# A trunk kernel with an expert layer: 64 columns of v move from dense products to gathered rows, and the weights are split two blocks at once

## The chip, the cores and the metric

The kernel runs on one core of a Trainium2 chip. The metric is the device time of one execution in microseconds (us), taken as the median of several executions. The profile names the engines PE (matmul; its weight loads are PEld), DVE (vector), ACT (scalar), POOL (GpSimd, which issues the gathers) and SP (which issues the plain loads).

## What is computed

The trunk has a mixing layer (a convolution and a state-space scan), cross attention to 256 memory tokens, an expert layer and a final norm, over 256 tokens of 2048 columns. The change lies in the last part, the expert layer's second half. For every token 8 heads x 16 experts are chosen out of 16384, each with a gate g and an activation act, and their rows of `v_tab` are added up:

```
def block(args):
    xt, it, gt = args
    u = jnp.take(u_tab, it, axis=0)
    act = jax.nn.gelu(jnp.einsum("td,tkd->tk", xt, u))
    v = jnp.take(v_tab, it, axis=0)
    return jnp.einsum("tk,tkd->td", gt * act, v)
...
h = h + peer(hn, peer_w_q[i], peer_keys[i], peer_u[i], peer_v[i])
...
return rms_norm(h, final_norm_g)
```

## The kernel before

The 256 tokens are two tiles of 128 (tt = 0 and 1). The sum over experts is made in two ways at once, split by columns.

**Dense columns.** The first DC = 1472 columns of v are a plain matrix product: W, a 16384 x 256 matrix of weights that is zero except where a token chose an expert, times `peer_v`. W lies ready in SBUF as two tiles, WA for tt = 0 and WB for tt = 1. The loop of lines 1199 to 1220 walks through 128 blocks of 128 experts. For each block ACT rounds 128 columns of WA and WB into `wh` (line 1205), DVE takes the rest into `wl` (line 1206), SP loads 128 rows of v into `vr` (line 1208), ACT rounds them into `vh` and DVE takes the rest into `vl` (`split`, lines 103 and 104). PE then adds three products (wh by vh, wl by vh, wh by vl; lines 1215 to 1217) for each token tile and each of three column pieces of 512, 512 and 448 columns: 18 matmuls a block, added up in PSUM tiles `acc` for the whole loop. `vr` has four buffers, `vh`, `vl`, `wh` and `wl` have two each.

**Gathered columns.** The last GC = 576 columns are gathered: for each of the 128 chosen experts of a token tile POOL issues one indirect DMA of 128 rows into `v` (line 1180, six buffers), and DVE adds them with their coefficients into `accg` (line 1182). That is 256 gathers and 256 additions. The text of the loop asks for them at a rate of (256 + 8) / 128 a block (line 1218).

**The end.** Lines 1222 to 1239 add `acc` to the residual h3 (which lies in used parts of WA and WB), square and sum the rows, take the root (`rstd_of`, line 110), scale and store. Each token tile needs all of its 128 gathers before the root.

**What sets the order.** The text is no order. When the program is built, a scheduler places every instruction on its engine's list by dependences, priorities and a timeline of its own; the chip then runs each engine's list strictly in order. So an instruction that waits holds up all that stands behind it on its engine, and a row that the scheduler placed late is run late, even if its data came long before.

## Time and profile before

| | us |
|---|---|
| median of 3 runs (2063.14 to 2064.17) | 2064.15 |
| the profiled execution, and its span | 2064.74, 2063.0 |
| first and last matmul of the dense products start | 1533.99, 2046.59 |
| busy in the span: PE, DVE, ACT, POOL | 1961.4, 1683.5, 998.2, 777.7 |

The last quarter of the span is the dense and gathered sum with the tail. The chain of work that ended last runs there through PE's `acc` lines, block after block, and behind the last of them mostly through DVE. The span is what lies between the first and the last instruction; the execution's own time is 1.74 us more.

### The profile page before, as it was taken

What the parts mean: (1) busy time and instruction counts of PE and PEld (TensorE: products, weight loads), DVE (VectorE), ACT (ScalarE), POOL (GpSimd) and SP (SyncE); (2) the same over time, 40 slices, a digit from 0 to 9 for tenths busy, and PEclk for the clock granted to TensorE, in tenths of its full rate; (3) what the DMA queues carried; (4) which work ended last, traced back from release to release, by engine and by line L of the source; (5) the groups of instructions that cost most, each with busy time, mean ns of one, the idle gap of its engine ahead of it and who ended that gap; (6) DMA issues with size and microseconds to landing.
All of it is one profiled execution on the core that took longest, in us unless ns stands there. A gap on an engine that the chain in (4) does not pass through costs nothing.

```text
span 2063.0 us, 33320 instructions
## 1 busy us (share of the span) xinstructions
PE 1961.4 (95%) x12361; PEld 1684.1 (82%) x12379; DVE 1683.5 (82%) x2757; ACT 998.2 (48%) x1586; POOL 777.7 (38%) x589
## 2 busy tenths in 40 slices
PE   8899999999999998899999989989999999999996
PEld 7888886786899888788888878867678888888885
DVE  6699999895655557999976666889869899899998
ACT  5775665455544445333333323556564444444444
POOL 1011111000000003444445656453128677677775
PEclk9999999999999999999999999999999999999998
DMA  7888788757855568899999999888539999999996
GB/s 238 204 227 221 202 224 223 226 183 230 276 180 173 168 196 280 273 310 327 318 354 398 406 384 407 282 294 280 172 128 338 364 336 340 343 341 338 337 339 228
DMA packets 203108, 571.78 MB, mean 277 GB/s; under 512 B 31410, under 2 KB 39459, under 8 KB 202818
## 3 DMA queue, kind: packets, MB, share of 16 engines
q1 hardware_dynamic: 135810, 307.48, 44.1%
q0 software_dynamic: 67136, 262.18, 37.8%
q8 instruction: 97, 1.59, 0.3%
q14 instruction: 65, 0.53, 0.1%
HBM read 556.74 MB, written 12.85 MB: 276 GB/s over the span
## 4 chain that ended last, share of the span: by engine, by line
PE 55%; DVE 15%; issue 11%; DMA 9%; POOL 7%; ACT 2%; SPq 0%; POOLq 0%; DVEq 0%; ACTq 0%
PE acc L1216 8%; PE acc L1217 8%; PE acc L1215 8%; POOL u L928 6%; DVE u L930 5%; PE mm L206 4%; PE mm L205 4%; PE mm L207 3%; PE mm L216 3%; PE mm L214 3%; PE mm L215 3%; PE pw L1051 3%; DMA w_lo<-in_w_kv_mem 2%; PE y L1016 1%; DMA xc<-in_mem 1%
## 5 line engine op out<-in xcount | busy, mean ns | idle before, releaser
L1180 POOL DMA_INDIRECT v<-in_peer_v,vidx x256 | 391.2, 1528 | 182.8 <-DVE accg L1182 72.5
L930 DVE SCALAR_TENSOR_TENSOR u<-u,hnF 128x1280 f32<-128x1280 f32 x256 | 387.9, 1518 | 86.2 <-DMA u<-in_peer_u,uidx 85.5
L928 POOL DMA_INDIRECT u<-in_peer_u,uidx x256 | 295.8, 1156 | 330.2 <-DVE u L930 243.3
L975 PE MATMUL sy<-hnT,ut 128*128 128x256 f32 x1536 | 357.6, 385 | 15.4 <-ACT ut L971 15.4
L191 ACT CAST w_hi<-w_raw 128x1024 fp32r<-128x1024 f32 (+2 forms) x228 | 231.3, 1017 | 242.8 <-PE mm L207 118.2
L975 PEld LDWEIGHTS sy<-hnT,ut 128*128 128x128 f32 x1536 | 287.6, 193 | 56.5 <-ACT ut L971 20.7
L196 DVE TENSOR_TENSOR w_lo<-w_raw,w_hi 128x1024 fp32r<-128x1024 f32 (+2 forms) x192 | 226.7, 1183 | 111.4 <-ACT w_hi L191 111.2
L103 ACT CAST vh<-vr 128x1472 fp32r<-128x1472 f32 x128 | 183.3, 1432 | 251.7 <-PE acc L1216 250.2
L1216 PE MATMUL acc<-vh,wl 128*128 128x512 f32 (+1 forms) x768 | 295.4, 385 | 0.3 <-DVE wl L1206 0.3
L1217 PE MATMUL acc<-vl,wh 128*128 128x512 f32 (+1 forms) x768 | 293.7, 385 | 0.1
L216 PE MATMUL mm<-aT_hi,w_lo 128*128 128x256 f32 x960 | 271.9, 290 | 18.8 <-DVE w_lo L196 7.5
L1215 PE MATMUL acc<-vh,wh 128*128 128x512 f32 (+1 forms) x768 | 276.0, 384 | 2.4 <-ACT vh L103 2.4
L214 PE MATMUL mm<-aT_hi,w_hi 128*128 128x256 f32 x960 | 277.1, 291 | 0.8 <-ACT w_hi L191 0.8
L215 PE MATMUL mm<-aT_lo,w_hi 128*128 128x256 f32 x960 | 274.4, 288 | 0.0
L104 DVE TENSOR_TENSOR vl<-vr,vh 128x1472 fp32r<-128x1472 f32 x128 | 216.8, 1694 | 41.9 <-ACT vh L103 41.4
L1182 DVE SCALAR_TENSOR_TENSOR accg<-v,coef,accg 128x576 f32<-128x576 f32 x256 | 208.7, 815 | 6.5 <-DMA v<-in_peer_v,vidx 2.5
L216 PEld LDWEIGHTS mm<-aT_hi,w_lo 128*128 128x128 f32 x960 | 182.8, 193 | 25.2 <-DVE w_lo L196 9.0
L214 PEld LDWEIGHTS mm<-aT_hi,w_hi 128*128 128x128 f32 x960 | 185.7, 194 | 6.6 <-issue 3.7
L215 PEld LDWEIGHTS mm<-aT_lo,w_hi 128*128 128x128 f32 x960 | 186.1, 194 | 3.4 <-issue 2.0
L1216 PEld LDWEIGHTS acc<-vh,wl 128*128 128x128 f32 x768 | 144.6, 188 | 30.9 <-DVE wl L1206 0.7
L1215 PEld LDWEIGHTS acc<-vh,wh 128*128 128x128 f32 x768 | 144.8, 188 | 28.3 <-ACT vh L103 2.6
L1217 PEld LDWEIGHTS acc<-vl,wh 128*128 128x128 f32 x768 | 144.5, 188 | 22.5 <-DVE vl L104 0.9
(383 smaller groups left out, 3187.8 us busy)
## 6 DMA issues: line engine op xcount, KB each, us to landing
vr<-in_peer_v SPq DMA_DIRECT2D x128, 736.0 KB
raw<-in_peer_u SPq DMA_DIRECT2D x128, 384.0 KB
w_raw<-in_w_kv_mem SPq DMA_DIRECT2D x64, 512.0 KB
w_raw<-in_w_in SPq DMA_DIRECT2D x48, 512.0 KB
w_raw<-in_w_out SPq DMA_DIRECT2D x32, 512.0 KB
w_raw<-in_w_q_mem SPq DMA_DIRECT2D x32, 512.0 KB
w_raw<-in_w_o_mem SPq DMA_DIRECT2D x32, 512.0 KB
w_lo<-in_w_kv_mem POOLq DMA_DIRECT2D x24, 512.0 KB, 7.9
```

Source lines behind the costliest of these rows:

```text
L191: S.copy(hi, raw)
L196: V.tensor_sub(lo, raw, hi.bitcast(F32))
L214: PE.matmul(o, wh, ah, start=first and cb % 2 == 0, stop=False, skip_group_check=True)
L215: PE.matmul(o, wh, al, start=False, stop=False, skip_group_check=True)
L216: PE.matmul(o, wl, ah, start=False, stop=last and end, skip_group_check=True)
L928: G.indirect_dma_start(out=u, out_offset=None, in_=a["peer_u"].rearrange("e (q c) -> (e q) c", c=GU), in_offset=bass.IndirectOffsetOnAxis( ...
L930: V.scalar_tensor_tensor(u, u, 1.0, hnF[:, self.tt, :], op0=ALU.mult, op1=ALU.mult, accum_out=self.act[:, j:j + 1])
L975: PE.matmul(ps[:, b % 2, :], ut[:, k, :], hnT[:, k, :], start=k == 0 and b % 2 == 0, stop=k == KD - 1 and b % 2 == 1, skip_group_check=True)
L1180: G.indirect_dma_start(out=v, out_offset=None, in_=table, in_offset=bass.IndirectOffsetOnAxis(ap=vidx[tt][:, j:j + 1], axis=0))
L1215: PE.matmul(o, wh[:, tt, :], vh[:, cs_], start=b == 0, stop=False)
L1216: PE.matmul(o, wl[:, tt, :], vh[:, cs_], start=False, stop=False)
L1217: PE.matmul(o, wh[:, tt, :], vl[:, cs_], start=False, stop=b == NB - 1)
```

## The change

Four things change in the text. GC goes from 576 to 640 and DC from 1472 to 1408, so that the column pieces are 512, 512 and 384, a block of `vr` has 704 KB instead of 736, and a gather 320 KB instead of 288. The weights are rounded and split for two blocks at a time: `wh` and `wl` are tiles of 2 x 128 columns, one for each token tile, in a ring of three buffers each that the two token tiles share. The products of tt = 1 for the last two blocks are written behind the loop. The gathers are asked for at (256 + 16) / 128 a block. Besides, a root of a constant, `eps_j`, is written ahead of the tail, and the option of splitting weights on POOL is gone.

```
--- before.py
+++ after.py
@@ -48,14 +48,14 @@
 DU = KD * P
 DG = D - DU
 GROUPS = ((1, 1, 2, 2, 2), (2, 2, 2, 2))
-GC = 576
+GC = 640
 GU = 64
 DC = D - GC
 COLS = [slice(c, min(c + 512, DC)) for c in range(0, DC, 512)]
 NCH = len(COLS)
 VG_BUFS = 6
 VR_BUFS = 4
-WL_POOL = 0
+WGROUP = 2
 PQ_COLS = (128, 384, 512)
 NWHOLE = 1
 W_IN, W_K, W_V = True, True, True
@@ -105,6 +105,8 @@
 
     def row_bcast(vec):
         return bass.AP(tensor=vec.tensor, offset=vec.offset, ap=[[0, P], [1, D]])
+
+    eps_j = consts.tile([P, 1], F32, name="eps_j")
 
     def rstd_of(dst, ssq, n):
         S.activation(dst, ssq, AF.Sqrt, bias=eps_t[: dst.shape[0]], scale=1.0 / n)
@@ -1196,28 +1198,41 @@
 
     gathering = gathered()
     done = 0
+
+    def products(b, tt, wh, wl, vh, vl):
+        for c, cs_ in enumerate(COLS):
+            o = acc[tt][:, c, :cs_.stop - cs_.start]
+            PE.matmul(o, wh, vh[:, cs_], start=b == 0, stop=False)
+            PE.matmul(o, wl, vh[:, cs_], start=False, stop=False)
+            PE.matmul(o, wh, vl[:, cs_], start=False, stop=b == NB - 1)
+
+    late = []
     for b in range(NB):
         if b == TAIL_AT:
             load_tail()
-        wh = vs.tile([P, NTT, P], F32R, name="wh")
-        wl = vs.tile([P, NTT, P], F32R, name="wl")
-        for tt in range(NTT):
-            S.copy(wh[:, tt, :], W[tt][:, b, :])
-            (G if tt < WL_POOL else V).tensor_sub(wl[:, tt, :], W[tt][:, b, :], wh[:, tt, :].bitcast(F32))
+            S.activation(eps_j, eps_t, AF.Sqrt)
+        i = b % WGROUP
+        if i == 0:
+            wh, wl = ([vs.tile([P, WGROUP, P], F32R, name=nm, bufs=3) for _ in range(NTT)] for nm in ("wh", "wl"))
+            for tt in range(NTT):
+                w = W[tt][:, b:b + WGROUP, :]
+                S.copy(wh[tt], w)
+                V.tensor_sub(wl[tt], w, wh[tt].bitcast(F32))
         vr = vraw_p.tile([P, DC], F32, name="vr")
         SY.dma_start(vr, a["peer_v"][b * P:(b + 1) * P, :DC])
         vh = vs.tile([P, DC], F32R, name="vh")
         vl = vs.tile([P, DC], F32R, name="vl")
         split(vh, vl, vr)
-        for tt in range(NTT):
-            for c, cs_ in enumerate(COLS):
-                o = acc[tt][:, c, :cs_.stop - cs_.start]
-                PE.matmul(o, wh[:, tt, :], vh[:, cs_], start=b == 0, stop=False)
-                PE.matmul(o, wl[:, tt, :], vh[:, cs_], start=False, stop=False)
-                PE.matmul(o, wh[:, tt, :], vl[:, cs_], start=False, stop=b == NB - 1)
-        while done * NB < (b + 1) * (NTT * NSLOT + 8) and done < NTT * NSLOT:
+        products(b, 0, wh[0][:, i, :], wl[0][:, i, :], vh, vl)
+        if b < NB - 2:
+            products(b, 1, wh[1][:, i, :], wl[1][:, i, :], vh, vl)
+        else:
+            late.append((b, 1, wh[1][:, i, :], wl[1][:, i, :], vh, vl))
+        while done * NB < (b + 1) * (NTT * NSLOT + 16) and done < NTT * NSLOT:
             next(gathering)
             done += 1
+    for x in late:
+        products(*x)
 
     sts = [small.tile([P, NCH + 3], F32, name="rms_st") for _ in range(NTT)]
     for tt, st in enumerate(sts):
```

What the build makes of it is seen in the engines' lists. Up to the first split of the weights they are the same but for one place: on ACT the root into `eps_j` and a table load for it stand at the very start of the kernel, the later table load for Exp (line 314 after) is new, and the table load of the tail is still there.

DVE, a steady block before (names with their numbers: `vl` is the split of a block, `accg1` the sum of the second token tile, `v` a gathered buffer):

```order
L104 TENSOR_TENSOR vl_18857<-vr_18854,vh_18856 128x1472
L1206 TENSOR_TENSOR wl_18849<-WA_8439,wh_18848 128x128
L1206 TENSOR_TENSOR wl_18849<-WB_7774,wh_18848 128x128
L1182 SCALAR_TENSOR_TENSOR accg1_14570<-v_18626,coef1_8417,accg1_14570 128x576
L1182 SCALAR_TENSOR_TENSOR accg1_14570<-v_18659,coef1_8417,accg1_14570 128x576
L104 TENSOR_TENSOR vl_18893<-vr_18890,vh_18892 128x1472
```

The same place after, somewhat more than two blocks:

```order
L104 TENSOR_TENSOR vl_18676<-vr_18673,vh_18675 128x1408
L1184 SCALAR_TENSOR_TENSOR accg1_14571<-v_17939,coef1_8418,accg1_14571 128x640
L104 TENSOR_TENSOR vl_18714<-vr_18711,vh_18713 128x1408
L1184 SCALAR_TENSOR_TENSOR accg1_14571<-v_17942,coef1_8418,accg1_14571 128x640
L1220 TENSOR_TENSOR wl_18706<-WB_7775,wh_18704 128x256
L1220 TENSOR_TENSOR wl_18764<-WA_8440,wh_18762 128x256
L1184 SCALAR_TENSOR_TENSOR accg1_14571<-v_17977,coef1_8418,accg1_14571 128x640
L104 TENSOR_TENSOR vl_18741<-vr_18738,vh_18740 128x1408
L1184 SCALAR_TENSOR_TENSOR accg1_14571<-v_17980,coef1_8418,accg1_14571 128x640
L1184 SCALAR_TENSOR_TENSOR accg1_14571<-v_18007,coef1_8418,accg1_14571 128x640
L104 TENSOR_TENSOR vl_18773<-vr_18770,vh_18772 128x1408
L1184 SCALAR_TENSOR_TENSOR accg1_14571<-v_18010,coef1_8418,accg1_14571 128x640
```

Before, each block has two additions of gathered rows and two splits of weights. After, the splits come once in two blocks, and in every four blocks there are seven additions, six of them seen here.

DVE, the end of the list before, around the root of the first token tile (`accg_14569` is that tile's sum, `accg_14570` the second's):

```order
L1182 SCALAR_TENSOR_TENSOR accg_14570<-v,coef_8417,accg_14570 128x576
L111 RECIPROCAL rms_st<-rms_st 128x1
L1182 SCALAR_TENSOR_TENSOR accg_14570<-v,coef_8417,accg_14570 128x576
L1237 SCALAR_TENSOR_TENSOR WA<-accg_14569,rms_st,WA 128x576
L1237 SCALAR_TENSOR_TENSOR WA<-WA,rms_st 128x512 x2
L1182 SCALAR_TENSOR_TENSOR accg_14570<-v,coef_8417,accg_14570 128x576
L1228 TENSOR_REDUCE rms_st<-rms_st 128x1
L111 RECIPROCAL rms_st<-rms_st 128x1
L1237 SCALAR_TENSOR_TENSOR WB<-accg_14570,rms_st,WA 128x576
L1237 SCALAR_TENSOR_TENSOR WB<-WB,rms_st,WA 128x512 x2
```

And after (`accg_14570` is the first tile's sum, `accg_14571` the second's):

```order
L113 RECIPROCAL rms_st<-rms_st 128x1
L1184 SCALAR_TENSOR_TENSOR accg_14571<-v,coef_8418,accg_14571 128x640
L1252 SCALAR_TENSOR_TENSOR WA<-accg_14570,rms_st,WA 128x640
L1252 SCALAR_TENSOR_TENSOR WA<-WA,rms_st 128x512 x2
L1184 SCALAR_TENSOR_TENSOR accg_14571<-v,coef_8418,accg_14571 128x640 x29
L1243 TENSOR_REDUCE rms_st<-rms_st 128x1
L113 RECIPROCAL rms_st<-rms_st 128x1
L1252 SCALAR_TENSOR_TENSOR WB<-accg_14571,rms_st,WA 128x640
L1252 SCALAR_TENSOR_TENSOR WB<-WB,rms_st,WA 128x512 x2
```

Behind the last `vl`, before has eight additions (three at once, then five singly among the rows of the tail), after has 35 (two, then four singly, then the 29 in one row here, all of the second token tile, whose root stands behind them). Up to the last `vl` it is 248 before and 221 after.

PE, where block 127 follows block 126, before (`acc_14567` is the first token tile's sum, `acc_14568` the second's), from the last row of block 126 on:

```order
L1217 MATMUL acc_14568<-vl_19133,wh_19124 128x448
L1215 MATMUL acc_14567<-vh_19162,wh_19154 128x512
L1215 MATMUL acc_14568<-vh_19162,wh_19154 128x512
L1216 MATMUL acc_14567<-vh_19162,wl_19155 128x512
L1217 MATMUL acc_14567<-vl_19163,wh_19154 128x512
L1215 MATMUL acc_14567<-vh_19162,wh_19154 128x512
L1216 MATMUL acc_14567<-vh_19162,wl_19155 128x512
L1217 MATMUL acc_14567<-vl_19163,wh_19154 128x512
L1215 MATMUL acc_14567<-vh_19162,wh_19154 128x448
L1216 MATMUL acc_14567<-vh_19162,wl_19155 128x448
L1217 MATMUL acc_14567<-vl_19163,wh_19154 128x448
L1216 MATMUL acc_14568<-vh_19162,wl_19155 128x512
```

And after, with `acc_14568` the first token tile's sum and `acc_14569` the second's, from the last rows of block 126 on the first tile to the second row of block 127:

```order
L1206 MATMUL acc_14568<-vh_18884,wl_18876 128x384
L1207 MATMUL acc_14568<-vl_18885,wh_18874 128x384
L1206 MATMUL acc_14569<-vh_18884,wl_18877 128x512
L1207 MATMUL acc_14569<-vl_18885,wh_18875 128x512
L1205 MATMUL acc_14569<-vh_18884,wh_18875 128x512
L1206 MATMUL acc_14569<-vh_18884,wl_18877 128x512
L1207 MATMUL acc_14569<-vl_18885,wh_18875 128x512
L1205 MATMUL acc_14569<-vh_18884,wh_18875 128x384
L1206 MATMUL acc_14569<-vh_18884,wl_18877 128x384
L1207 MATMUL acc_14569<-vl_18885,wh_18875 128x384
L1205 MATMUL acc_14568<-vh_18899,wh_18874 128x512
L1206 MATMUL acc_14568<-vh_18899,wl_18876 128x512
```

In both the second token tile's products of a block follow at once on the first tile's: block 126's second tile stands ahead of block 127, though the text puts it behind.

## Rows read from the trace of the kernel before

**Rows 1.** Stretch of the stage: its length, busy PE, PEld, DVE, ACT, POOL; clock, DMA
```profile
1900.00:1960.00 60.00, 60.00 (x272) 50.88 (x271) 54.90 (x76) 27.60 (x46) 46.63 (x31) 1.00 0.94 334
```

**Rows 2.** Chain of waits near the end: start, us, what
```profile
2031.01 0.47 PE acc L1215 x2
...
2032.62 0.20 PE acc L1215
...
2033.23 0.23 PE acc L1216
...
2042.97 0.47 PE acc L1215 x2
```

**Rows 3.** Timeline of DVE, one block: start, us, what, idle time before it
```profile
1801.08 1.69 DVE L104 TENSOR_TENSOR vl<-vr,vh 128x1472 fp32r<-128x1472 f32 x1 [0.30 <-ACT vh L103]
1802.69 0.28 DVE L1206 TENSOR_TENSOR wl<-WA,wh 128x128 fp32r<-128x128 f32 x1
...
1803.10 1.67 DVE L1182 SCALAR_TENSOR_TENSOR accg<-v,coef,accg 128x576 f32<-128x576 f32 x2
1805.11 1.69 DVE L104 TENSOR_TENSOR vl<-vr,vh 128x1472 fp32r<-128x1472 f32 x1 [0.34 <-ACT vh L103]
```

**Rows 4.** Timeline of all engines at the end
```profile
2042.30 2.52 DVE L1182 SCALAR_TENSOR_TENSOR accg<-v,coef,accg 128x576 f32<-128x576 f32 x3
2045.22 1.82 DVE L1225 TENSOR_TENSOR WA<-WA,acc 128x512 f32<-128x512 f32 x3 [0.41 <-PE acc L1217]
2046.59 0.36 PE L1217 MATMUL acc<-vl,wh 128*128 128x448 f32 x1
2052.86 0.81 DVE L1237 SCALAR_TENSOR_TENSOR WA<-accg,rms_st,WA 128x576 f32<-128x576 f32 x1
2054.91 0.81 DVE L1182 SCALAR_TENSOR_TENSOR accg<-v,coef,accg 128x576 f32<-128x576 f32 x1
```

**Rows 5.** Timeline of PE in an earlier stage, matmuls of 256 columns
```profile
641.03 0.28 PE L216 MATMUL mm<-aT_hi,w_lo 128*128 128x256 f32 x1
...
642.95 0.28 PE L214 MATMUL mm<-aT_hi,w_hi 128*128 128x256 f32 x1
```

**Rows 6.** Groups by line and shape from 1440 us on: busy, mean ns | idle
```profile
L1237 DVE SCALAR_TENSOR_TENSOR WA<-WA,rms_st 128x512 f32<-128x512 f32 x2 | 1.4, 746 | 0.0
L1237 DVE SCALAR_TENSOR_TENSOR WA<-accg,rms_st,WA 128x576 f32<-128x576 f32 x1 | 0.8, 812 | 0.0
L1225 DVE TENSOR_TENSOR WA<-WA,acc 128x512 f32<-128x512 f32 x2 | 1.3, 684 | 0.4 <-PE acc L1217 0.4
L1225 DVE TENSOR_TENSOR WA<-WA,acc 128x448 f32<-128x448 f32 x1 | 0.6, 614 | 0.0
```

**Rows 7.** The page's costliest groups, gathers and the rounding of v
```profile
L1180 POOL DMA_INDIRECT v<-in_peer_v,vidx x256 | 391.2, 1528 | 182.8 <-DVE accg L1182 72.5
L103 ACT CAST vh<-vr 128x1472 fp32r<-128x1472 f32 x128 | 183.3, 1432 | 251.7 <-PE acc L1216 250.2
```

**Rows 8.** Timeline of POOL at the start of the stage
```profile
1538.79 0.95 POOL L1180 DMA_INDIRECT v<-in_peer_v,vidx  x1 [0.31 <-issue]
1540.05 0.95 POOL L1180 DMA_INDIRECT v<-in_peer_v,vidx  x1 [0.30 <-DVE accg L1182]
1541.30 0.95 POOL L1180 DMA_INDIRECT v<-in_peer_v,vidx  x1 [0.30 <-issue]
```

**Rows 9.** DMA issues from 2038 us on: KB each, median us to landing
```profile
v<-in_peer_v,vidx POOLq DMA_INDIRECT x5, 4.0
```

**Rows 10.** Timeline of ACT at the kernel's start
```profile
14.93 0.20 ACT L312 ACTIVATE dtt<-ldt 32x2 f32<-32x2 f32 x1
19.46 0.64 ACT L253 ACTIVATE sqj<-xc 128x512 f32<-128x512 f32 x1 [4.33 <-DMA xc<-in_x]
```

**Rows 11.** Busy time of each engine while u's rows are gathered
```profile
1340.00:1360.00 20.00, 19.94 (x252) 16.68 (x251) 20.00 (x32) 12.05 (x22) 9.29 (x10) 1.00 0.94 320
```

**Rows 12.** Timeline of POOL in that stretch
```profile
1346.48 0.94 POOL L928 DMA_INDIRECT u<-in_peer_u,uidx  x1 [1.07 <-DVE u L930]
```

## The prediction

> **What bounds the kernel now.** I read the stretches of the last stage first. In 60 us of it PE is busy for all 60, at full clock, DVE for 54.9, and the DMA engines move 334 GB/s [rows 1]. So PE sets the pace there, with DVE close behind it. The chain of waits gives the pace: three blocks of v take 2042.97 - 2031.01 = 11.96 us, 3.987 us a block [rows 2]. In it seven matmuls of 512 columns take 1.61 us (0.230 each) and the next three, of 448, take 0.61 us (0.203 each). DVE's row of one block is a split of v that holds it for 1.61 us (1801.08 to 1802.69), two splits of weights for 0.41, two additions of gathered rows for 1.67, then a wait of 0.34 for the next `vh` [rows 3]. That is 3.69 of 3.99 us. Last I read the tail. The last product starts at 2046.59 and ends about 2046.8; call that E. DVE adds up the first token tile from 2045.22 on, scales it from 2052.86 on, adds its last gathered row at 2054.91 = E + 8.1, and the span ends 8.1 us behind that [rows 4]. Before E only PE counts; behind it only DVE's list, and what that waits for.
>
> **The narrower dense products.** Six of a block's 18 matmuls go from 448 to 384 columns. Their price lies between two rows: 16 matmuls of 256 columns follow one another in 1.92 us, 0.120 each [rows 5], those of 448 take 0.203, so a column costs 0.083 / 192 = 0.434 ns, and 384 columns take 0.1755. That also shows that the weight load in between is no floor at 384, since it is none at 256. By the step from 448 to 512 a column costs 0.42 ns, which gives 20.5 us in all; I take the rows around 384: 6 x 0.0278 = 0.167 us a block, 3.82 instead of 3.987, and 128 x 0.167 = **21.3 us** off PE. All of it lies on the path as long as nothing else in the block needs 3.82 us.
>
> **Does DVE keep up?** 64 columns cost DVE 66 to 70 ns [rows 6]. So the split of v falls to 1.54 us, an addition rises to 0.90, and one split of 256 weight columns in place of two of 128 takes 0.205 + 0.14 = 0.345, twice in two blocks, so 0.345 a block instead of 0.41. The list after has 7 additions in 4 blocks, not 8: 1.54 + 0.345 + 1.75 x 0.90 = 3.46 us. DVE keeps up with 0.36 us to spare. What makes that room is that the list puts 27 additions fewer ahead of the last split of v (221 for 248), and those come back below. Bytes change little: 721 KB of `vr` and 1.75 x 328 KB gathered are 1.294 MB in 3.82 us, 339 GB/s, for 334 measured now [rows 1].
>
> **A new wait on ACT.** The two token tiles' `wh` share a ring of three buffers. The WA tile of the next pair therefore waits for the end of the odd block, where PE last reads the WB tile three places before it. Behind it on ACT stands the `vh` of the pair's second block, behind that DVE's `vl`, behind that PE. From the end of the odd block on: about 0.1 us to wake, at most 0.4 for the rounding of 256 columns, 1.4 for `vh` [rows 7], 0.3 to DVE's start [rows 3], 1.54 for `vl`, 3.7 us in all. PE wants that `vl` at the fifth matmul of the next block, 3.82 + 4 x 0.23 = 4.74 us later. The wait is covered by a block of PE's work, with 1 us left, and I set it at nothing. If that cover were gone, a pair would lose up to the rounding, 0.35 us, 64 times: 22 us.
>
> **The last two blocks by token tile** change nothing: PE's list still has the second tile of block 126 ahead of block 127, so the first tile's sum ends about 1.6 us ahead of E, as now (2045.22 is 1.6 us before 2046.8). Cost 0.
>
> **The early root** stands at the kernel's start and spares no table load in the tail. It adds a load there, ahead of Exp at 14.93, where ACT then idles 4.33 us for a DMA [rows 10]. It would have to be longer than that to be seen; without the idle time it would cost its whole length. Cost 0.
>
> **The gathered rows end later, not sooner.** Between E and the end of the first tile's scaling both lists have four single additions, so DVE is through with it at E + 8.1 to E + 8.2 in either. Before, one addition is left then. After, 29 are, with the second tile's root behind them. The six `v` buffers hold landed rows by then, so six additions run at 0.90 us. The seventh needs a gather that can start only when the first frees its buffer, at E + 9.1. POOL issues a gather every 1.25 us when nothing holds it (1538.79, 1540.05, 1541.30: 0.95 of work and 0.30 between) [rows 8], and DVE frees buffers faster than that. So the 23rd gather starts at E + 9.1 + 22 x 1.25 = E + 36.6. In the tail a gather lands 4.0 us from its issue [rows 9], 4.1 with 320 KB; the ring of six stands 6 x 1.25 - 0.9 = 6.6 us of that, so landing does not set the pace. The last addition starts at E + 40.7 instead of E + 8.1: 32.6 us later, and 0.2 more for its width and those of the square and scaling behind it: **32.8 us** on the path.
>
> Bounds of this term. Below: DVE alone, 28 x 0.90 behind E + 8.2, last start E + 33.4, 25.5 us. Above: the mean gather of the loaded stage, 1.53 + 0.30 = 1.83 us [rows 7], 22 of them: 45.5 us. I take 1.25: nothing but gathers is loaded by then, and 328 KB in 1.25 us are 262 GB/s, well under the 334 of the stage [rows 1], so nothing should hold POOL back.
>
> **The sum:** -21.3 + 32.8 = +11.5 us on the profiled execution, 2064.74 to 2076.2. The median of the runs is 0.6 us lower, so I forecast 2075.7, rounded to **2076 us**, 0.6% slower.
>
> **Rivals.**
> 1. *The gathers in the tail keep their loaded pace* of 1.83 us. For it: it is the mean of 256. Against it: those stood behind loads of `vr`. It gives 2064.15 - 21.3 + 45.5 = 2088.
> 2. *DVE sets the tail's pace.* For it: DVE has the work in a row. Against it: no two gathers in the trace start closer than 1.25 us. 2064.15 - 21.3 + 25.5 = 2068.4, at the edge of what can be told from no change.
> 3. *ACT's wait reaches PE* (above). For it: three buffers for two tiles. Against it: 1 us of cover. 2076 + 22 = 2098.
> 4. *DVE's additions hold up POOL.* If an addition, which reads two tiles in SBUF, kept POOL from starting, a gather would take up to 0.9 us more: 22 x 0.9 = 20 us, 2096. Against it: while u's rows are gathered DVE is busy for 20.00 of 20 us with an operation of that form, two inputs in SBUF [rows 11], and a gather takes 0.94 us [rows 12], as it does beside a mostly idle DVE [rows 8]. The Trainium skill ("SBUF — State Buffer", section "Who interferes with whom") has a rule that a vector instruction with two SBUF inputs contends with a GpSimd instruction that reads SBUF, the later of the two blocking fully; rows 11 and 12 do not show it for gathers.
> 5. *The other side: the gathers keep the text's rate*, 2.125 a block, and end at block 121. DVE would need 1.54 + 0.345 + 2.125 x 0.90 = 3.80 us, just under 3.82, and the tail would lose its five additions and the wait for the last, some 5 us: 2064.15 - 21.3 - 5 = 2038. The sign turns where DVE's list has some 26 additions or fewer behind the last split, since 11.5 us are 9 gathers of 1.25 us less than the 35. Against it: the list has 35, and the list of before agrees with its trace (three additions from 2042.30 on, then singly).
>
> **How the numbers follow.** Forecast 0.75; rival 1 0.10; 2 0.04; 3 0.03; 4 0.03; 5 0.05. About 0.2% (4 us) is what a measurement of this kernel can tell from no change. Rival 5 is faster, 0.05; half of rival 2 is the same and the rest, 0.93, slower; I put 0.03 on the same for small errors of both large terms that add up, and leave 0.92. The forecast's own range is 2072 to 2081 (1.25 to 1.45 us a gather, 1 us of PE's term either way). To hold 8 in 10 it reaches to rival 2 below and rival 1 above: 2068 to 2088.
>
> **What would show it.** PE's blocks 3.82 us apart with `acc` never waiting for `vl` or `wl`; the last product 21 us earlier, about 2025.5; then some 29 additions in a row on DVE, the first six back to back, the rest 1.25 us apart and waiting for the DMA of `v`; POOL's gathers 0.95 us long there; the span's end 49 us behind the last product, where it is 16 now. Wrong would be: gathers over 1.4 us long in the tail, blocks longer than 3.9 us, or a list on the chip without the long run of additions.

## The result

Over four runs each the changed kernel takes 2082.7 us (2081.4 to 2084.9) and the kernel before 2063.6 (2062.5 to 2064.2): 1.0089 times as long, 95% interval 1.0073 to 1.0105. It is slower by 19 us, where 12 were forecast. The forecast's sign and place hold: PE needs less time and the tail grows by more than that. But each of the two terms was off, and one reason given for the tail was wrong.

The profiled run of after took 2084.86 us with a span of 2083.1. Its first product of `acc` and its last ones, in PE's row of operations (start, duration, engine, line, operation, idle time ahead of it and what ended it):

```profile
1536.65 0.50 PE L1205 MATMUL acc<-vh,wh 128*128 128x512 f32 x1 [2.24 <-ACT vh L103]
...
2031.67 0.33 PE L1205 MATMUL acc<-vh,wh 128*128 128x384 f32 x1
2031.84 0.34 PE L1206 MATMUL acc<-vh,wl 128*128 128x384 f32 x1
2032.02 0.34 PE L1207 MATMUL acc<-vl,wh 128*128 128x384 f32 x1
```

Matmuls of 384 columns start 0.17 to 0.18 apart, so E, the end of the products, is 2032.2 here (2046.8 before, by [rows 4]). DVE's row behind it is what the prediction described, a run of additions that wait for `v`:

```profile
2039.37 1.41 DVE L1252 SCALAR_TENSOR_TENSOR WA<-WA,rms_st 128x512 f32<-128x512 f32 x2
2040.69 4.56 DVE L1184 SCALAR_TENSOR_TENSOR accg<-v,coef,accg 128x640 f32<-128x640 f32 x5
2046.28 0.89 DVE L1184 SCALAR_TENSOR_TENSOR accg<-v,coef,accg 128x640 f32<-128x640 f32 x1 [1.03 <-DMA v<-in_peer_v,vidx]
...
2074.96 0.88 DVE L1184 SCALAR_TENSOR_TENSOR accg<-v,coef,accg 128x640 f32<-128x640 f32 x1 [0.26 <-issue]
2076.74 0.16 DVE L1243 TENSOR_REDUCE rms_st<-rms_st 128x1 f32<-128x4 f32 x1 [0.90 <-ACT WB L1242]
```

The stretches of the stage answer [rows 1]. Columns are the stretch, the busy time of PE, its weight loads, DVE, ACT and POOL, then granted clock, DMA share and GB/s. The last row is the tail, where PE does nothing for 35 us:

```profile
1800.00:1900.00 100.00, 100.00 (x471) 86.23 (x470) 89.66 (x99) 45.81 (x54) 64.55 (x45) 1.00 0.93 339
2040.00:2075.00 35.00, 0.00 (x0) 0.00 (x0) 25.49 (x31) 0.00 (x0) 24.36 (x24) 0.50 0.82 259
```

So a profiled run falls into three parts: up to the stage's first product, from there to E, and from E to the end of the span. The table has them for all profiles, in us; "behind" is how many additions stand behind the last split of `v` in DVE's order. The first three columns are of the one profiled run of a kernel, the last is the median of its runs. For x4 the two differ most: its profiled run took 2090.6 us, 8 more than the median.

| kernel | first product | to E | tail | behind | median of runs |
|---|---|---|---|---|---|
| before | 1534.0 | 512.8 | 16.2 | 8 | 2063.6 |
| after | 1536.7 | 495.5 | 50.9 | 35 | 2082.7 |
| x1 width alone | 1532.3 | 496.2 | 54.9 | 33 | 2084.4 |
| x2 pairs alone | 1535.3 | 513.7 | 17.2 | 10 | 2067.4 |
| x3 two a block | 1532.1 | 521.7 | 13.9 | 2 | 2069.3 |
| x4 three loads | 1536.3 | 538.6 | 14.0 | 0 | 2082.8 |
| x5 second tile later | 1534.6 | 498.6 | 14.0 | 2 | 2046.0 |
| x6 x1, sum in PSUM | 1532.8 | 496.5 | 46.9 | 32 | 2078.9 |
| x7 x5, sum in PSUM | 1533.0 | 498.5 | 14.0 | 2 | 2047.6 |
| x8 x5 with 576 | 1534.4 | 515.3 | 14.0 | 2 | 2065.2 |
| x9 x5, late blocks | 1530.8 | 499.5 | 10.7 | 2 | 2044.0 |
| x10 x5 with 704 | 1531.7 | 476.9 | 14.0 | 2 | 2027.2 |
| x11 x9 with 704 | 1534.9 | 478.6 | 12.6 | 2 | 2027.3 |

The runs of the kernel before that stand beside the experiments have medians of 2063.2 to 2064.5 and spread from 2059 to 2071, so each experiment's ratio to them is given below, with its 95% interval. How far apart blocks are is taken from the starts of successive roundings of `v` into `vh`. In the code cuts `...` marks lines left out.

### The profile page after: what moved, and what is told of

Its sections match the earlier page's. It is cut to its first block, busy times and chain, and to the rows that moved or that the text cites. A ratio compares the mean times of both kernels' runs of the same rounds, so it can differ in the third digit from the quotient of the medians.

```text
span 2083.1 us, 32994 instructions
## 1 busy us (share of the span) xinstructions
PE 1942.8 (93%) x12361; PEld 1673.4 (80%) x12379; DVE 1682.0 (81%) x2629; ACT 987.5 (47%) x1460; POOL 739.0 (35%) x589
## 3 DMA queue, kind: packets, MB, share of 16 engines
q1 hardware_dynamic: 135810, 303.29, 42.8%
## 4 chain that ended last, share of the span: by engine, by line
PE 53%; DVE 15%; issue 12%; DMA 10%; POOL 7%; ACT 2%; SPq 0%; POOLq 0%; DVEq 0%; ACTq 0%
PE acc L1207 8%; PE acc L1206 8%; PE acc L1205 8%; POOL u L930 7%; DVE u L932 5%; PE mm L218 4%; PE mm L217 3%; PE mm L216 3%; PE mm L208 3%; PE mm L207 3%; PE mm L209 3%; PE pw L1053 3%; DMA w_lo<-in_w_kv_mem 2%; DMA xc<-in_mem 1%; PE y L1018 1%
## 5 line engine op out<-in xcount | busy, mean ns | idle before, releaser
L1182 POOL DMA_INDIRECT v<-in_peer_v,vidx x256 | 359.2, 1403 | 238.0 <-DVE accg L1184 138.3
L930 POOL DMA_INDIRECT u<-in_peer_u,uidx x256 | 289.0, 1129 | 337.4 <-DVE u L932 252.3
L1205 PE MATMUL acc<-vh,wh 128*128 128x512 f32 (+1 forms) x768 | 288.5, 376 | 2.9 <-ACT vh L103 2.9
L1206 PE MATMUL acc<-vh,wl 128*128 128x512 f32 (+1 forms) x768 | 287.6, 375 | 0.0
L1207 PE MATMUL acc<-vl,wh 128*128 128x512 f32 (+1 forms) x768 | 277.7, 375 | 2.1 <-DVE vl L104 2.1
L103 ACT CAST vh<-vr 128x1408 fp32r<-128x1408 f32 x128 | 175.9, 1374 | 145.0 <-PE acc L1206 137.9
L104 DVE TENSOR_TENSOR vl<-vr,vh 128x1408 fp32r<-128x1408 f32 x128 | 208.0, 1625 | 37.0 <-ACT vh L103 33.9
L1184 DVE SCALAR_TENSOR_TENSOR accg<-v,coef,accg 128x640 f32<-128x640 f32 x256 | 225.5, 881 | 14.9 <-DMA v<-in_peer_v,vidx 9.4
```

The lines of the kernel that those rows point to most:

```text
L930: G.indirect_dma_start(out=u, out_offset=None, in_=a["peer_u"].rearrange("e (q c) -> (e q) c", c=GU), in_offset=bass.IndirectOffsetOnAxis( ...
L1182: G.indirect_dma_start(out=v, out_offset=None, in_=table, in_offset=bass.IndirectOffsetOnAxis(ap=vidx[tt][:, j:j + 1], axis=0))
L1184: V.scalar_tensor_tensor(accg[tt], v, coef[tt][:, j:j + 1], accg[tt], op0=ALU.mult, op1=ALU.add)
L1205: PE.matmul(o, wh, vh[:, cs_], start=b == 0, stop=False)
L1206: PE.matmul(o, wl, vh[:, cs_], start=False, stop=False)
L1207: PE.matmul(o, wh, vl[:, cs_], start=False, stop=b == NB - 1)
```

## The experiments

**x1: the width alone.**

```diff
-GC = 576
+GC = 640
```

> The kernel before with 640 gathered columns for 576 and nothing else of the change. Its order has 33 additions behind the last split of v (8 before the change, 35 after it). My theory: each addition behind the end of PE's products costs one issue of a gather, 1.25 us (1.33 as the tail of the changed kernel measured), and the width gives PE's gain. So blocks 3.82 to 3.84 us apart, the last product some 15 us earlier than before, and the time 2.5 us under the changed kernel's 2082.7, since two additions are fewer: 2080. Rival (the weights split two blocks at once cost PE something through their shared ring of three): then PE's blocks are shorter here than the changed kernel's 3.836, and the time is 2076 or less. Rival (the long run of additions comes of the paired splits): then the time is near 2050, which the order speaks against.

Measured: 2084.4 us, 1.0082 (1.0053 to 1.0112), where 2080 were forecast. To E it needs 496.2 us, as the changed kernel does (495.5). So the paired splits give PE nothing and take nothing, and the 64 columns alone bring both the gain and the run of additions. But the tail is 4 us longer than after's, with two additions fewer. Its gathers start 1.65 us apart (20 intervals from 2037.99 to 2070.89), against 1.33 in after (22 intervals from 2041.84 to 2071.03). POOL's row of that tail, then DVE's of the same time:

```profile
2051.30 1.41 POOL L1180 DMA_INDIRECT v<-in_peer_v,vidx  x1 [0.30 <-issue]
2053.01 1.57 POOL L1180 DMA_INDIRECT v<-in_peer_v,vidx  x1 [0.30 <-DMA v<-in_peer_v,vidx]
2054.89 0.95 POOL L1180 DMA_INDIRECT v<-in_peer_v,vidx  x1 [0.30 <-issue]
2056.14 1.37 POOL L1180 DMA_INDIRECT v<-in_peer_v,vidx  x1 [0.30 <-issue]
...
2051.01 0.88 DVE L1182 SCALAR_TENSOR_TENSOR accg<-v,coef,accg 128x640 f32<-128x640 f32 x1 [0.83 <-DMA v<-in_peer_v,vidx]
2052.86 0.88 DVE L1182 SCALAR_TENSOR_TENSOR accg<-v,coef,accg 128x640 f32<-128x640 f32 x1 [0.97 <-DMA v<-in_peer_v,vidx]
2054.07 0.89 DVE L1182 SCALAR_TENSOR_TENSOR accg<-v,coef,accg 128x640 f32<-128x640 f32 x1 [0.33 <-DMA v<-in_peer_v,vidx]
2055.80 0.88 DVE L1182 SCALAR_TENSOR_TENSOR accg<-v,coef,accg 128x640 f32<-128x640 f32 x1 [0.85 <-DMA v<-in_peer_v,vidx]
```

Read them in pairs. The gather of 2053.01 starts while the addition of 2052.86 has 0.73 us to go, and takes 1.57. That of 2056.14 finds 0.54 us left and takes 1.37. That of 2054.89 finds 0.07 left and takes 0.95. All 18 gathers from 2043 on fit 0.95 us plus what is left of the running addition, less about 0.1. This is rival 4, which the prediction had all but thrown out (0.03).

**x2: the paired splits alone.**

```diff
+WGROUP = 2
...
-        wh = vs.tile([P, NTT, P], F32R, name="wh")
...
+        if i == 0:
+            wh, wl = ([vs.tile([P, WGROUP, P], F32R, name=nm, bufs=3) for _ in range(NTT)] for nm in ("wh", "wl"))
...
```

> The kernel before with the weights split two blocks at once and nothing else of the change. Its order has 10 additions behind the last split of v, 8 before. My theory: the shared ring of three weight tiles costs PE nothing, blocks stay 3.987 us apart, and two more additions in the tail cost 2 x 1.3 us: 2063.6 + 2.6 = 2066. Rival (ACT's wait for the ring reaches PE): up to 0.35 us in each of 64 pairs, 2066 + 22 = 2088, with PE waiting at the first matmul of every second block. On the 2.7 us by which the changed kernel was late already ahead of the stage: this kernel has no early square root, so if that caused them, the stage's first product starts at 1534.0 as before; if they are spread between executions, it may start anywhere from 1533 to 1537.

Measured: 2067.4 us, 1.0000 (0.9984 to 1.0017), so no difference that can be told. PE waits for nothing from 1540 on, and blocks are 3.987 us apart but for the first ten (4.07). The tail is 1.0 us longer for two more additions. The stage starts at 1535.3 without an early root. Over all 13 profiles the start lies between 1530.8 and 1536.7; nine with the root average 1533.8, four without it 1533.6. So the 2.7 us by which the profiled run of after was late ahead of the stage are spread between executions.

**x3: two additions behind every split.** DVE's order is fixed as the loop is written, and the loop hands out two gathers a block.

```diff
+    in_order.enter_context(tc.manual_schedule(engines={mybir.EngineType.DVE}))
     for b in range(NB):
...
-        while done * NB < (b + 1) * (NTT * NSLOT + 16) and done < NTT * NSLOT:
+        while done * NB < (b + 1) * (NTT * NSLOT) and done < NTT * NSLOT:
```

> The changed kernel with DVE's order in the last stage written out: behind every split of v two additions of gathered rows, so that 2 stand behind the last split instead of 35. Nothing else differs. My theory: DVE needs 1.625 + 0.345 + 2 x 0.881 = 3.73 us a block, by the means of the changed kernel, PE 3.836, so the blocks stay as they are, the last product starts near 2032, and the tail falls from 50.7 us behind it to about 9 (no gather left to wait for): 2082.7 - 41 = 2042, faster than both. Rival (DVE or the gathers can't hold two a block beside everything else): the blocks lengthen to the 3.99 of before or more, the last product ends near 2052 and the time is 2062 or later. Rival (the loss sits in wider gathers and additions as such, not in their place): 2070 or later.

Measured: 2069.3 us, 1.0019 (1.0005 to 1.0033); the forecast of 2042 failed. The tail shrank as expected, from 50.9 to 13.9 us. But blocks are 4.04 us apart, and DVE's row of two blocks says why:

```profile
1801.03 0.42 DVE L1222 TENSOR_TENSOR wl<-WA,wh 128x256 fp32r<-128x256 f32 x1
1802.25 0.45 DVE L1222 TENSOR_TENSOR wl<-WB,wh 128x256 fp32r<-128x256 f32 x1 [0.80 <-ACT wh L1221]
1802.62 1.61 DVE L104 TENSOR_TENSOR vl<-vr,vh 128x1408 fp32r<-128x1408 f32 x1
1804.16 1.79 DVE L1184 SCALAR_TENSOR_TENSOR accg<-v,coef,accg 128x640 f32<-128x640 f32 x2
1805.87 1.62 DVE L104 TENSOR_TENSOR vl<-vr,vh 128x1408 fp32r<-128x1408 f32 x1
1807.40 1.80 DVE L1184 SCALAR_TENSOR_TENSOR accg<-v,coef,accg 128x640 f32<-128x640 f32 x2
1809.12 0.42 DVE L1222 TENSOR_TENSOR wl<-WA,wh 128x256 fp32r<-128x256 f32 x1
...
1809.90 0.41 ACT L1221 CAST wh<-WB 128x256 fp32r<-128x256 f32 x1 [1.13 <-PE acc L1207]
```

From 1801.03 to 1809.12 there is no idle time but 0.80 us: 7.29 us of work and a wait for the second tile's `wh`, which ACT rounds only when PE has released a buffer of the ring of three. That is the wait of rival 3, reaching PE by another engine: with DVE's order fixed, the next split of `v` queues behind it.

**x4: three buffers for the loads of v.** By the order this makes the additions run ahead, 2.3 a block, and end at block 112.

```diff
-VR_BUFS = 4
+VR_BUFS = 3
```

> The changed kernel with three buffers for the loads of v instead of four. By the order this makes additions run ahead: 2.3 a block up to block 112 and none behind that, so none stands behind the last split. My theory: up to block 112 DVE needs 1.625 + 0.345 + 2.29 x 0.881 = 3.99 us and sets the pace, then PE with 3.83: 112 x 3.99 + 16 x 3.83 = 508 us for the stage instead of 495.5, last product near 2044.5, tail 9 us: 2055. So slower than the order with two a block by some 12 us and faster than both kernels. Rival (four buffers are needed to hide the loads of v): PE waits for vh on a DMA, blocks above 4.1 us, 2070 or later. Rival (only PE's pace and the number behind the end count, DVE's load doesn't): 2042, as the order with two a block.

Measured: 2082.8 us, 1.0084 (1.0060 to 1.0107); the forecast of 2055 failed by 28. No addition is left in the tail, and the stage takes 43 us longer than after's in the profiled run (the slowest of four; by the medians some 8 us less). POOL's gathers and DVE's work of one stretch:

```profile
1803.46 1.23 POOL L1182 DMA_INDIRECT v<-in_peer_v,vidx  x1 [0.30 <-issue]
1805.61 2.09 POOL L1182 DMA_INDIRECT v<-in_peer_v,vidx  x1 [0.92 <-DVE accg L1184]
1808.00 1.41 POOL L1182 DMA_INDIRECT v<-in_peer_v,vidx  x1 [0.31 <-DVE accg L1184]
...
1805.25 1.62 DVE L104 TENSOR_TENSOR vl<-vr,vh 128x1408 fp32r<-128x1408 f32 x1
1806.79 2.72 DVE L1184 SCALAR_TENSOR_TENSOR accg<-v,coef,accg 128x640 f32<-128x640 f32 x3
...
1813.79 0.89 DVE L1184 SCALAR_TENSOR_TENSOR accg<-v,coef,accg 128x640 f32<-128x640 f32 x1 [0.48 <-DMA v<-in_peer_v,vidx]
```

Ten gathers start in 18.46 us (1798.87 to 1817.33), 1.85 us each; 2.29 of them a block make 4.23 us, about what the blocks take (3.9 to 4.7 in stretches of ten up to block 110). The gathers are late because DVE holds them up (that of 1805.61 starts 0.36 us into a split of 1.62), and the additions, which stand ahead of the next split, wait for them, 27 us in all between 1540 and 2010 where after has 2.4. Loads of `v` are waited for once, 2.3 us; whether three buffers cost something besides was not separated.

**x5: the second tile's split behind the next split of v.** In x3's order one step moves.

```diff
...
-                V.tensor_sub(wl[tt], w, wh[tt].bitcast(F32))
+                if tt == 0:
+                    V.tensor_sub(wl[tt], w, wh[tt].bitcast(F32))
...
         split(vh, vl, vr)
+        if i == 0:
+            V.tensor_sub(wl[1], w, wh[1].bitcast(F32))
...
```

> As x3 (two additions behind every split of v, 2 behind the last), with one step of DVE moved: the weight split of the second token tile stands behind the next split of v, no longer ahead of it. In x3 DVE's list is 7.28 us of work for two blocks and a wait of 0.80 for the second tile's rounded weights, which ACT can round only when PE is through with the first tile's old ones (three buffers for both): 8.08 us, PE's 7.67 is no longer the bound. My theory: that wait is what made x3 slow. Behind the next split the weights are there, DVE needs 7.28 for two blocks, PE sets the pace again with 3.836 a block, 495.5 us from the first to the last product, and x3's tail of 13.9 us: 2045, faster than both kernels. Rival (the bytes are the bound: 721 + 656 = 1377 KB a block): at the 355 GB/s that x3 reached in its fastest 100 us a block takes 3.88 us, 2051; at the 343 GB/s of the changed kernel 4.01 us, 2068, and the split of v waits for a DMA. Rival (gathers held up by DVE come too late for two a block): DVE waits for v at its additions.

Measured: 2046.0 us, 0.9912 (0.9890 to 0.9933), faster than both kernels, and 2045 were forecast. Blocks are 3.836 us apart from the eleventh on. DVE's row again:

```profile
1807.68 0.42 DVE L1223 TENSOR_TENSOR wl<-WA,wh 128x256 fp32r<-128x256 f32 x1
1808.25 1.62 DVE L104 TENSOR_TENSOR vl<-vr,vh 128x1408 fp32r<-128x1408 f32 x1 [0.15 <-ACT vh L103]
1809.84 0.42 DVE L1230 TENSOR_TENSOR wl<-WB,wh 128x256 fp32r<-128x256 f32 x1
1810.19 1.80 DVE L1184 SCALAR_TENSOR_TENSOR accg<-v,coef,accg 128x640 f32<-128x640 f32 x2
```

The stretches, with the columns as above:

```profile
1600.00:1700.00 100.00, 100.00 (x471) 86.19 (x470) 95.46 (x105) 45.26 (x53) 79.89 (x53) 1.00 0.98 375
1800.00:1900.00 100.00, 100.00 (x471) 86.19 (x470) 95.66 (x106) 45.24 (x53) 79.83 (x53) 1.00 0.97 361
```

The wait of 0.80 is gone, PE is busy throughout with DVE at 95.5%, and the DMA engines move 361 to 375 GB/s. So neither the bytes nor the gathers bind here. Only the first ten blocks are slow (4.34 each, 5 us in all): the first addition waits 3.10 us for its start value from memory and the second 2.18 us for its gather, and in a fixed order the splits wait behind them.

**x6 and x7: the running sum in PSUM**, in x1 and in x5.

```diff
+    accp = psg.tile([P, 1024], F32, name="accp")[:, :GC]
...
+            V.tensor_copy(accp, accg[tt])
...
-                V.scalar_tensor_tensor(accg[tt], v, coef[tt][:, j:j + 1], accg[tt], op0=ALU.mult, op1=ALU.add)
+                V.scalar_tensor_tensor(accp, v, coef[tt][:, j:j + 1], accp, op0=ALU.mult, op1=ALU.add)
+                if j == NSLOT - 1:
+                    V.tensor_copy(accg[tt], accp)
```

> x1 (the kernel before with 640 gathered columns), with the running sum of the gathered rows held in PSUM instead of SBUF: an addition then reads one tile in SBUF and one in PSUM, and 32 stand behind the last split. In x1's tail a gather takes 0.95 us plus what is left of the addition that DVE is in the middle of when it starts (1.47 with 0.66 us left, 0.95 with 0.07), 1.73 us from start to start. Theory (an addition that reads two tiles in SBUF holds up a gather that starts behind it; the rule of the Trainium skill, SBUF - State Buffer, Who interferes with whom): here no gather of the tail is longer than about 0.96 us, they start 1.25 apart, and 19 x 0.48 = 9 us and one addition go: 2074. Rival (the tail's gathers are slowed by memory or by their queue): they keep 1.1 to 1.57 us and the time is 2082 or more. The predicted text had thrown this cause out.

> x5 with the running sum in PSUM as in x6. If PE sets x5's pace: 2045 as x5, within 2 us, with gathers of 0.95 us wherever no split of v runs at their start. If x5 waits for gathers that DVE holds up: faster than x5 by that wait. If an addition that reads PSUM is slower than 0.88 us by more than 0.1, DVE passes PE's pace and it is slower than x5.

Measured for x6: 2078.9 us, 1.0075 (1.0053 to 1.0097), 5.5 us under x1 and 5 over the forecast of 2074; in the profiles the tail is 8.0 us shorter. The forecast's 9 us for the gathers took 19 steps of 1.73 us; by x1's 20 steps of 1.65 it is 20 x 0.40 = 8, and the one addition less is nearly made up for by a copy of 0.82. POOL's and DVE's rows of its tail:

```profile
2054.44 0.95 POOL L1184 DMA_INDIRECT v<-in_peer_v,vidx  x1 [0.30 <-issue]
2055.69 0.95 POOL L1184 DMA_INDIRECT v<-in_peer_v,vidx  x1 [0.30 <-issue]
...
2060.69 0.94 POOL L1184 DMA_INDIRECT v<-in_peer_v,vidx  x1 [0.30 <-issue]
...
2060.15 1.81 DVE L1186 SCALAR_TENSOR_TENSOR accp<-v,coef,accp 128x640 f32<-128x640 f32 x2 [0.69 <-DMA v<-in_peer_v,vidx]
```

The last 20 gathers all take 0.94 to 0.96 us, and from 2040.66 on they start 1.25 apart, whatever DVE is doing. One that starts 0.54 us into an addition (2060.69, the first of the two additions from 2060.15 on) takes 0.94 too. In x6's stage the splits of `v`, whose two inputs are still in SBUF, go on holding gathers up (2.13 us at 1900.51, 1.30 us ahead of a split's end). The same engine, the same instruction and the same bytes: what decides is whether DVE's running instruction reads two tiles in SBUF. (x6 moves what the addition writes out of SBUF as well. That this is not it is seen in the kernel before, at `H<-H,y`, further down: it reads one tile in SBUF and writes one, and holds no gather up.) That is the rule of the Trainium skill ("SBUF — State Buffer", section "Who interferes with whom"): a vector instruction with two SBUF inputs and a GpSimd instruction that reads SBUF contend, and the later one blocks. The traces agree where the gather is the later one, 0.95 us without and up to 1.57 with it in the tail. They do not show it the other way round: an addition that starts while a gather runs keeps its 0.88 to 0.89 us.

x7 takes 2047.6 us, 0.9915 (0.9889 to 0.9942), as x5: there PE sets the pace, and gathers held up a little cost nothing. An addition takes 0.886 us with its sum in PSUM and 0.882 without.

**x8: x5's order with the 576 columns of before.**

```diff
-GC = 640
+GC = 576
```

> x5 with the 576 gathered columns of before: pairs of blocks and DVE's order as there, no column moved. PE needs 3.987 us a block, 512.8 us in all; 754 + 590 = 1344 KB a block are 337 GB/s. Theory (PE sets the pace in both): last product where before has it, tail 13.9 instead of 16.3 us, 2062; and the distance to x5 is what the 64 columns are worth when the additions keep up, 17 us (128 x 0.15 less what the tail's width costs). Rival (the bytes are the bound): x5 and this come within 8 us of each other.

Measured: 2065.2 us, 1.0007 (0.9992 to 1.0022). The tail is 2.2 us shorter than before's and the first ten blocks, at 4.24 us, give that back. The distance to x5 is 19 us: that is what the 64 columns are worth when no addition is left over (17 were forecast here, and the prediction had put PE's gain at 21.3).

**x9 to x11: the last two blocks really by tile, and 64 columns more.** In x9 PE's order of blocks 126 and 127 is fixed too; x10 is x5 with `GC = 704`; x11 is both.

```diff
...
+        if b == NB - 2:
+            in_order.enter_context(tc.manual_schedule(engines={mybir.EngineType.PE}))
         products(b, 0, wh[0][:, i, :], wl[0][:, i, :], vh, vl)
...
```

> x5 with PE's order of the last two blocks written out too, so that the first token tile takes both blocks before the second takes either: what the change's last two blocks were meant to be, and what the order of the changed kernel does not have (there block 127 of the first tile still stands behind block 126 of the second). Theory: the first tile's sum then ends 3.8 us before the last product instead of 1.6, its scaling and root leave the tail, and of x5's 13.9 us behind the last product some 9 to 11 remain; PE may lose up to 0.7 us where block 127 now asks for its split of v half a block earlier. 2046 - 3 = 2043, a difference at the edge of what can be told in time and plain in the trace (the first tile's additions of acc on DVE start 3.8 us before the last product's end). Rival (PE loses what the tail gains): 2046.

> x5 with 704 gathered columns for 640: 64 more go the way of the change. PE 3.836 - 0.167 = 3.67 us a block. DVE (3.64 in x5) loses 0.07 at the split of v and gains 2 x 0.07: 3.71. Bytes: 688 + 721 = 1409 KB, 380 GB/s at 3.71 us, 375 was the most in 100 us of x5. Theory: DVE or the DMAs now bind before PE, so the step is worth less than the last: DVE's bound gives 128 x (3.836 - 3.71) = 16 us, 2030; the 361 GB/s that x5 moved from 1800 to 1900 would give 3.90 us a block, 8 us slower than x5, 2054. I expect a value between, 2036 to 2048, with PE waiting for vl. Rival (PE still binds): 2046 - 21 = 2025.

> x9 and x10 together. If they add up: x10 less the 3 us of x9. If DVE or the DMAs bind in x10, PE has slack there, and the order of the last two blocks costs PE nothing.

Measured: x9 2044.0 us, 0.9907 (0.9886 to 0.9928); x10 2027.2, 0.9828 (0.9809 to 0.9846); x11 2027.3, 0.9813 (0.9794 to 0.9832). x9's tail is 10.7 us, 3.3 shorter, and PE waits 0.57 us for a split of `v` in its last blocks: as forecast, though the gain in time isn't told apart from nothing. In x11 the tail is 1.4 us shorter than x10's and the stage 1.7 longer (PE waits 1.55 us for the last block's split of `v`), so the two do not add up. x10 beats its forecast of 2036 to 2048. Its stretches:

```profile
1600.00:1700.00 100.00, 99.99 (x492) 84.29 (x491) 97.84 (x109) 45.55 (x54) 77.53 (x55) 1.00 1.01 395
1800.00:1900.00 100.00, 100.00 (x495) 84.44 (x494) 99.05 (x111) 46.30 (x56) 78.68 (x56) 1.00 1.00 387
```

Blocks are about 3.65 us apart, with PE at 100%, DVE at 99% and the DMA share at 1.00, all at once. My 3.71 for DVE was too dear, since it added up durations, and instructions that follow one another overlap by some 0.08 us. Behind the start-up PE waits once, 0.32 us for `vl`, and its matmuls follow one another at 0.232 us (512 columns) and 0.145 (320), which make up the 3.65 by themselves. So PE still sets the pace, which was the rival of the expectation (2025), with next to nothing left on DVE and the DMA engines.

## Why the prediction was right, and where it was off

The time lies in the range of 2068 to 2088 that was to hold 8 in 10, and above the narrower 2072 to 2081 that the forecast gave itself for small errors of its own terms.

**PE's term: -21.3 forecast, -17.3 measured.** Two things are missing. Blocks are 3.836 us apart, not 3.82, which is 0.151 us a block and 19.3 in all. The narrow products came out as forecast, 0.176 us apart (0.1755), and save 0.161 of the 0.167; the twelve of 512 columns, which the sum left as they were, start 0.2317 us apart where before has 0.2308. And two stretches of ten blocks take 39.7 us for 38.4, 2.6 us that the step "A new wait on ACT" had set at nothing (the start-up took back 0.6). The rows of one of them, on ACT, then on PE:

```profile
1621.63 0.41 ACT L1219 CAST wh<-WB 128x256 fp32r<-128x256 f32 x1 [4.53 <-PE acc L1207]
1621.94 1.37 ACT L103 CAST vh<-vr 128x1408 fp32r<-128x1408 f32 x1
...
1623.36 0.50 PE L1205 MATMUL acc<-vh,wh 128*128 128x512 f32 x1 [0.31 <-ACT vh L103]
```

ACT idles 4.53 us for a buffer of the shared ring with `vh` queued behind it, and PE stands still for `vh`. In the regular pattern the cover that the prediction worked out holds, since PE waits nowhere else behind the start-up; at two places the order puts the second tile's rounding ahead of a `vh` that is wanted sooner. The prediction weighed the mechanism rightly for one pattern and took it for all 64 pairs. But the shared ring is not needed for such a place. x1, which splits block by block into two buffers, has one too: ACT waits 3.33 us for a buffer of `wh` with `vh` behind it, and PE loses the same 2.6 us there (ten blocks in 41.0 us for 38.4, at 1624). So what costs is a place on ACT's list that comes without the pairs as well.

**DVE keeps up, the early root, the late blocks.** DVE kept up: PE waits 2.1 us for `vl` in the whole stage, 0.70 us at the most, and 0.9 of it stands behind the two late `vh` above. The root costs nothing that shows. The last two blocks change nothing, since the order doesn't carry them out (DVE starts adding `acc` at 2030.94 here, E - 1.3); x9 shows what they would have brought, 3.3 us of tail.

**The tail: 32.8 forecast, 34.7 measured** (50.9 for 16.2). The last addition starts at E + 42.8, forecast E + 40.7. The 22 gathers behind the first freed buffer took 29.2 us for 27.5. The step's size was nearly right and its reason wrong. "Nothing but gathers is loaded by then", the prediction said, "so nothing should hold POOL back", and so laid the long gathers of the stage to memory. They are long because DVE is in the middle of an instruction. Of the first four gathers behind the first freed buffer in after three are held up, two of them over the 1.4 us that the prediction had named as a sign of being wrong:

```profile
2041.84 1.47 POOL L1182 DMA_INDIRECT v<-in_peer_v,vidx  x1 [0.91 <-DVE accg L1184]
2043.62 1.53 POOL L1182 DMA_INDIRECT v<-in_peer_v,vidx  x1 [0.31 <-DVE accg L1184]
2045.45 0.95 POOL L1182 DMA_INDIRECT v<-in_peer_v,vidx  x1 [0.30 <-DVE accg L1184]
2046.71 1.28 POOL L1182 DMA_INDIRECT v<-in_peer_v,vidx  x1 [0.30 <-issue]
2048.30 0.95 POOL L1182 DMA_INDIRECT v<-in_peer_v,vidx  x1 [0.31 <-DVE accg L1184]
```

From 2048.30 on a gather finds at most 0.2 us of an addition left as it starts, so steps of 1.25 to 1.31 us hold from there. In x1 the additions start just ahead of the gathers, and the steps are 1.65 us on average. Which of the two comes seems to hang on when rows land against POOL's beat; no run tests that (x1's four runs lie 7.7 us apart and x6's 1.6, but kernels without such a tail spread as widely). The rule "1.25" was luck to that extent, and rival 4, at 0.03, was the mechanism with the phase left out. Rival 2 falls, since DVE waits for `v` through the tail. Rival 1's 2088 lies a little nearer to the 2082.7 than the forecast's 2076 does, but its pace of 1.83 us and its cause, memory, are not what the trace shows.

**Why rival 4 was thrown out.** [Rows 11, 12] show DVE busy for 20.00 of 20 us beside gathers of 0.94. The row of operations tells more: what was running at the instant a gather starts (kernel before, POOL, then DVE, at one place in that stretch and at one 26 us later):

```profile
1346.48 0.94 POOL L928 DMA_INDIRECT u<-in_peer_u,uidx  x1 [1.07 <-DVE u L930]
...
1372.41 1.95 POOL L928 DMA_INDIRECT u<-in_peer_u,uidx  x1 [6.30 <-DVE u L930]
...
1346.13 0.68 DVE L1023 TENSOR_TENSOR H<-H,y 128x512 f32<-128x512 f32 x1
1346.73 1.49 DVE L930 SCALAR_TENSOR_TENSOR u<-u,hnF 128x1280 f32<-128x1280 f32 x1
...
1372.06 1.49 DVE L930 SCALAR_TENSOR_TENSOR u<-u,hnF 128x1280 f32<-128x1280 f32 x1
```

At 1346.48 DVE is in `H<-H,y`, whose `y` lies in PSUM; the instruction with two SBUF inputs begins 0.25 us later. At 1372.41 the gather starts 0.35 us into that instruction, and takes 1.95. A busy share can't show that two instructions never met. The trace of before could have settled it: 36 gathers of `u` start in `H<-H,y` with over 0.3 us of it left and take 0.93 to 0.94; of 60 that start so in `u<-u,hnF`, 53 take 0.8 us plus what is left, up to 2.26 (the other seven start within 0.05 us of its start), and so do all 99 gathers of `v` that start so in an addition of the stage, 1.28 to 1.56.

**Rival 5**, the other side of zero, was right as a mechanism and is what x5 does: 2046 with two additions a block, 2038 forecast. Its condition, what DVE's order holds behind the last split, sets the tail in every run (46.9 us and more with 32 to 35 behind, 14.0 and less with 0 to 2). x3 and x4 show that it is not enough, since an order without additions left over can also put a wait ahead of the split that PE needs next.

**The sum.** 2.7 us of the profiled difference lie ahead of the stage and are not put down to the change, since over the 13 profiles the stage's start scatters by 6 us with no sign of the root in it (x2); 4.0 are PE's term and 1.9 the tail's. Together they are the 8.6 us by which the span of 2083.1 exceeds the forecast one.

## What to carry to other kernels

A narrower product pays on the engine that binds only as long as the work moved elsewhere still ends with it: count what stands behind the last dense step in the emitted order of every engine, and fix that order if a scheduler's differs. In a fixed order look at what each instruction waits for, since all behind it on its engine waits too; moving one 0.4 us split behind the next large one was worth 23 us here (x3 to x5). And before taking an instruction's loaded duration for a matter of memory, set it beside what the neighbour engine is doing at the instant it starts.

## What the hardware showed unexpectedly

- A gather's issue on POOL takes 0.95 us, and up to 2.44 (in before) when DVE is in an instruction with two SBUF inputs as it starts; DVE's own instruction keeps its length (0.88 to 0.89 for an addition in either tail). With one of the inputs in PSUM the gather keeps 0.95. Over the 13 traces 3181 gathers are held with over 0.3 us of such an instruction left, and all but one take 0.80 to 0.84 us plus what is left. The one, 3.49 us at 1555.49 in after, stays unexplained. A gather that starts within 0.05 us of DVE's instruction can escape (159 such take 0.95).
- The DMA engines moved 395 GB/s over 100 us in x10, where 339 to 347 GB/s in after's stage stand at a share of 0.92 to 0.94 already.
- A running sum in PSUM costs DVE 0.004 us more on 640 columns than one in SBUF.
